# An opening stage with hand-ordered loads and all four weight folds, in a two-layer hybrid diffusion step

## The chip, the cores and the metric

The kernel runs on one core of one Trainium2 chip. The metric is the device time of one execution in microseconds (us); of several runs the median counts. The engines are TensorE (PE in the profile, with its weight loads apart as PEld), VectorE (DVE), ScalarE (ACT), GpSimd (POOL) and SyncE (SP), which issues every data transfer (DMA) of this kernel. Each engine takes its instructions in one order, which is fixed when the program is built.

## What is computed

One inference step with two layers over 1024 latent and 256 context tokens, 1024 wide. Cut to what matters here:

```python
for l in range(2):
    shift, scale, gate = split3(silu(cvec) @ ada_w[l] + ada_b[l])   # for c and for c_ctx
    h = rms_norm(x, norm_g[l]) * (1 + scale) + shift
    if l == 0:   # two attentions: A over all keys, B in a window, both also over cached context keys
        qa, ka, va, ga, qb, kb, vb, gb = split(h @ w_in)
        oa = attention(rope(rms(qa)), rope(rms(ka)), va)
        ob = window_attention(rope(qb), rope(kb), vb, sink)
        y = concat([oa * silu(ga), ob * silu(gb)]) @ w_out
    else:        # Fourier mixing in 4 groups of 256 channels
        u, g = split2(h @ odd_w_in)
        y = (real(fft2(u by group)) * silu(g)) @ odd_w_out
    x = x + gate * y
return rms_norm(x, final_g), new_keys_and_values
```

## The kernel before

**Tiles and precision.** The tokens are ten tiles of 128 rows (0 to 7 latent, 8 and 9 context), in three groups: 0 (tiles 0 to 3), 1 (4 to 7), 2 (8 and 9). Most products are made in three matmuls of high and low parts (hi x hi, hi x lo, lo x hi), so weights and activations are split into a high and a low tile.

**Conditioning.** `cs` holds SiLU of the two conditioning vectors. `ada_load(kk)` fetches four pieces of 512 KB of `ada_w` for layer 0, a chunk of 256 channels; `ada_chunk` multiplies them into a bank and fills scale and shift (`moda`, `modb`) of two of the eight 128-channel blocks k. The other three thirds that are made early (the gate of layer 0, shift and scale of layer 1) come in 24 `ada_step`s of one 512 KB load each, which `ada_fill(n)` issues in portions.

**Weight folds.** The transform of Fourier mixing along a group's 256 channels is multiplied into the projection weights: fold g is `wuT` rows of group g (1 MB) times the constant table `fch`. `fold_load(g)` fetches the rows, `fold_piece(g, kb2)` makes a quarter of the fold: eight matmul records of 256 columns, a copy to a buffer by ScalarE, a store to `wd` in DRAM. `wd` is read much later, in the second layer. Four folds of four pieces are to be made at some time before.

**The opening.** With `EF = 1` fold 0 is made first, its four stores being kept in `later`. Then a loop over the blocks k = 0 to 7 handles group 0: loads of `ada_w`, key weights (at `AT_K`) and query weights (at `AT_Q`), the norm of the group's rows (`norm_rows(0)`, one reciprocal root for all four tiles), `raw_T(0)`, which transposes x into eight banks and copies them to buffers, `mod_chunk` with scale and shift, and, three blocks behind, `gemm_chunk` into four open banks `acc0`: keys and queries of tile pairs 0 and 2. x of groups 1 and 2 is loaded there as well.

The list `S1` then names what follows, in order: `n` norm and `m` modulate a group, `c` cached keys, `K` and `Q` finish an open pair (norm, rotary positions, split), `k` and `q` project a pair and finish it. `AT_N` says how many `ada_step`s go ahead of each. Posts (transposes and stores of a finished pair) are held back two deep (`fl_.depth = 2`). Scratch for finished pairs comes from the buffer kinds in `HZ[0]`.

**Filler in the attentions.** Units of attention A, then of B, run in `attend`; after each, `fl_.pump` gives credit and the filler issues queued work in the order of `ORDER`: query pairs, key pairs of B, fold 1 (`f1`), gate columns. `FLATE = "f2 f3"` puts folds 2 and 3 behind the output weights. Behind these stand the output projection's steps (`proj_load`, `proj_step`), the first four row blocks of which may run inside attention B, once the tiles they read are finished for some units and seven buffers of the kinds u and w are free (`can_run`).

**Who sets the order.** The source order is not the engines' order: a planner at build time lists the instructions by priority in source order, with a timeline of its own, and may put a later ready instruction ahead of an earlier one. Buffers are named rings (`ZONES`: "h" 9, "u" 26, "w" 8, "p" 4, "pt" 3, "q" 2, "e" 4); a load into a buffer waits for that buffer's last reader, and everything behind it on SP waits too. PSUM has eight banks: "s" and "t" three each, "a" and "g" one each.

Matmuls of line 547 in the profile are fold pieces, 471 conditioning, 408 transposes of x, 523 the projections of the opening's loop, 257 all other products in parts, 895 and 967 scores, 1012 and 1018 attention weights and output. Line 831 issues the loads of `ada_step`, 498 those of `ada_load`, 900 the loads of queries from `qd`.

Of the kernel before, what the change touches and what calls it, by code (L numbers as in the profile page):

```python
# [57 lines left out]
ORDER = "qa0 qa1 kb0 qb0 qb1 f1 f0 g0 g1 g2 g3"  # L58
FLATE = "f2 f3"
# [74 lines left out]
def hybrid_step(ctx: ExitStack, tc: tile.TileContext, I, O):  # L134
# [143 lines left out]
    def load_w(src, width=256, tags="w", gap=None, lc=E_WL, each=None):  # L278
        out = []
        for kp in range(2):  # L280
            hi = take(tags, (P, 4, width), F32R)
            lo = take(tags, (P, 4, width), F32R)
            for j in range(2):
# [11 lines left out]
                split(hi[:, 2 * j : 2 * j + 2, :], lo[:, 2 * j : 2 * j + 2, :], raw.a, XE["wh"], lc)  # L295
                drop(raw)
# [95 lines left out]
    def norm_rows(gi):  # L392
        xs = XS[gi]
        n = len(xs)
        ssq = sm.tile([P, 4], F32, tag="ssq", name=f"n{gi}q")
        for i, x in enumerate(xs):
            junk = take("h", (P, D), BF16)
            act.activation(junk.a, x.a, AF.Square, accum_out=ssq[:, i : i + 1])
            drop(junk)
        rs = rsqrt(f"n{gi}r", ssq[:, 0:n], n, 1.0 / D, pw=PW[0])  # L400
        for i, x in enumerate(xs):
            dve.tensor_scalar(x.a, x.a, rs[:, i : i + 1], None, op0=ALU.mult)
# [10 lines left out]

    def raw_T(gi):
        raws = []
        for s in range(4):
            ht = take("u", (P, 2, 512))
            for j in range(2):
                copy("rawT", "ad", ht[:, j, :], x_T(gi, 2 * s + j))
            raws.append(ht)  # L420
        drop(*XS[gi])
        return raws
# [26 lines left out]

    def modulate(gi, lc):  # L450
        h_alloc(gi)
        for k in range(8):
            hh, hl = h_slot(gi, k)
            src = x_T(gi, k)
            tmp = take("h", src.shape)
            mod_chunk(gi, k, src, tmp.a, hh, hl, lc)
            drop(tmp)
        drop(*XS[gi])
# [33 lines left out]
    def ada_load(kk):  # L492
        out = []
        for hb in range(2):
            for part in range(2):
                raw = take(("p", "pt", "q"), (P, 4, 256))
                c0 = part * D + kk * 256
                sp.dma_start(
                    raw.a, I["ada_w"][0, hb * 512 : hb * 512 + 512, c0 : c0 + 256].rearrange("(b p) c -> p b c", p=P)
                )  # L500
                out.append(raw)
        return out

    def ada_chunk(kk, raws):
# [6 lines left out]
        drop(*raws)  # L511

        def fill(tv):
            mod_shift(0, 2 * kk, 2, tv[:, 0:2])
            mod_scale(0, 2 * kk, 2, tv[:, 2:4])

        ada_mods(0, f"modt{kk}", ps, fill)
# [13 lines left out]
    def fold_load(g):  # L531
# [3 lines left out]
        wu = []  # L535
        for j in range(2):
# [4 lines left out]
    def fold_piece(g, kb2, wu, tag="g", later=None):  # L541
        f = fold["f"]
        acc = bank(tag, f"wa{g}{kb2}")
# [6 lines left out]
        wo = take("u" if later is not None else "h", (P, 2, 256))  # L550
        copy("wo", "a", wo.a, acc.rearrange("p (i f) -> p i f", i=2))

        def put():
            rows = slice(kb2 * 256, kb2 * 256 + 256)
            sp.dma_start(wd[g // 2, rows, g % 2, :].rearrange("(k p) f -> p k f", p=P), wo.a)
            drop(wo)

        if later is None:
            put()
        else:  # L560
            later.append(put)
# [7 lines left out]
    early, later = [], []  # L569
    if XF:  # L570
        load_x(0, "u")
    for g in range(EF):
        early.append(fold_load(g))
    if not XF:
        load_x(0, "u")
    for g in range(EF):
        for k in range(4):
            fold_piece(g, k, early[g], "t", later)
    sp.dma_start(gT, I["gT"])
    sp.dma_start(bT, I["bT"])  # L580
    dve.tensor_scalar(bT1, bT[:, :, 8:16], 1.0, None, op0=ALU.add)
    h_alloc(0)
    acc0 = {("k", t): bank("s", f"kv{t}s") for t in (0, 2)}
    acc0.update({("q", t): bank("sa"[t // 2], f"q{t}s") for t in (0, 2)})
    wka = wqa0 = None
    for k in range(8):
        if k % 2 == 0:
            ada = ada_load(k // 2)
        if k == AT_K:
            wka = load_w(w0cols(C_KA), lc=LC0)  # L590
        if k == AT_Q:
            wqa0 = load_w(w0cols(C_QA), lc=LC0)
# [3 lines left out]
        if k == AT_X:  # L596
            load_x(1, "u")
        if k == 0:
            norm_rows(0)
            raws = raw_T(0)  # L600
        if k % 2 == 0:
            ada_chunk(k // 2, ada)
        hh, hl = h_slot(0, k)
        src = raws[k // 2][:, k % 2, :]
        mod_chunk(0, k, src, src, hh, hl, "dp")
        if k % 2 == 1:
            drop(raws[k // 2])
        for j in range(k - GL if k < 7 else k - GL, k - GL + 1 if k < 7 else 8):
            if j < 0:
                continue  # L610
            for nm, at, w in (("k", AT_K, wka), ("q", AT_Q, wqa0)):
                if j >= at:
# [1310 lines left out]
```

## Time and profile before

| what | value |
|---|---|
| median of 3 runs | 1216.64 us (1215.78 to 1218.63) |
| the profiled execution | 1214.73 us |
| its span | 1212.9 us |
| mean granted TensorE clock | 0.991 |
| first matmul (fold 0) | 5.57 us |
| first scores of attention A | 117.37 us |
| fold 1 on TensorE | 445.79 to about 463 us |
| folds 2 and 3 | 705.21 to 743 us |
| first matmul of the output projection | 747.80 us |
| last matmul of attention B | 813.98 us |

A row of the profile's groups gives the line, engine and operation, output and inputs by the program's names, shapes and count; then busy time and the mean of one in ns; then idle time of the engine just before, and what ended it. In the timeline, neighbours of one kind are merged into a row with the start, the length and the count; brackets hold the idle time before and its releaser. In the view of waits a row names who waited, for whom, the total in us, the times and the longest. The view by windows counts, in each stretch, the busy time and the instructions of each engine, the granted clock, the mean busy share of the 16 DMA engines and the GB/s moved. A matmul that stands waiting for its input in the array's pipeline may count as busy.

### The profile page before, as it was taken

Reading aid. Unit: us, or ns where it says so; the run is one execution under the profiler, and the core shown is the slowest. Engines: PE = TensorE matmul, PEld = TensorE weight load, DVE = VectorE, ACT = ScalarE, POOL = GpSimd, SP = SyncE. Lnnn points to the kernel's source line nnn. Section 1 sums busy time; section 2 is a strip of 40 time slices with the busy share of each in tenths; the row PEclk is TensorE's granted clock in tenths of the full one; section 3 lists DMA queues with packets and bytes.
Section 4 is the critical chain, followed back from the end, with each engine's and each line's share of the span. In section 5 each row is a group of like instructions: output and inputs, shape, how many; then the busy total and the mean of one; then the engine's idle time right before and its main releaser. Section 6 shows DMA issues by size and latency. Waiting matters only on the chain. (4 is left out here: it accounts for less than half of the span.)

```text
span 1212.9 us, 22074 instructions
## 1 busy us (share of the span) xinstructions
PE 1162.7 (96%) x8103; PEld 1038.2 (86%) x8103; DVE 842.6 (69%) x1997; ACT 580.5 (48%) x1163; POOL 321.9 (27%) x277
## 2 busy tenths in 40 slices
PE   7879999999999999999999989999999999999997
PEld 5768889999999998999988877877787888997886
DVE  4388888877786785668888867586765953368543
ACT  4352466555565465556667765532365224342211
POOL 2264543503321231010110113311312217344001
PEclk9999999999999999999999999999999999999999
DMA  9947312323524233344343688477214434354321
GB/s 334 369 165 268 88 59 76 93 86 98 139 60 132 78 112 92 91 124 123 84 122 102 190 211 237 150 235 211 103 39 141 153 113 141 123 191 159 122 103 54
DMA packets 129328, 168.81 MB, mean 139 GB/s; under 512 B 26298, under 2 KB 86454, under 8 KB 129220
## 3 DMA queue, kind: packets, MB, share of 16 engines
q1 hardware_dynamic: 129220, 167.40, 44.3%
q8 instruction: 64, 1.05, 0.4%
q14 instruction: 44, 0.36, 0.1%
HBM read 123.19 MB, written 44.16 MB: 138 GB/s over the span
## 5 line engine op out<-in xcount | busy, mean ns | idle before, releaser
L1015 DVE TENSOR_TENSOR pt<-pt,pt 128x512 fp32r<-128x512 f32 (+1 forms) x264 | 170.3, 658 | 45.5 <-ACT pt L269 44.9
L269 ACT ACTIVATE pt<-pt 128x512 fp32r<-128x512 f32 (+1 forms) x264 | 146.2, 576 | 87.9 <-PE pt L1012 55.9
L1018 PE MATMUL av<-pt,u 128*128 128x256 f32 x1008 | 169.9, 290 | 0.6 <-DVE e L1029 0.3
L1012 PE MATMUL pt<-identr,p 128*128 128x128 f32 x1008 | 155.0, 273 | 3.1 <-DVE pt L1015 1.6
L1018 PEld LDWEIGHTS av<-pt,u 128*128 128x128 f32 x1008 | 140.3, 189 | 5.1 <-DVE pt L1015 0.9
L257 PE MATMUL q<-w,u 128*128 128x256 f32 x864 | 132.8, 289 | 1.5 <-DVE u L433 1.5
L1012 PEld LDWEIGHTS pt<-identr,p 128*128 128x128 f32 x1008 | 118.6, 141 | 9.6 <-DVE pt L1015 2.6
L257 PE MATMUL ga<-u,w 128*128 128x512 f32 (+1 forms) x576 | 124.2, 360 | 0.1
L257 PEld LDWEIGHTS q<-w,u 128*128 128x128 f32 x864 | 116.1, 191 | 6.2 <-DVE u L433 1.9
L936 ACT ACTIVATE p<-p,nm 128x1280 f32<-128x1280 f32 (+1 forms) x80 | 95.3, 1191 | 53.3 <-DVE p L929 49.8
L257 PEld LDWEIGHTS ga<-u,w 128*128 128x128 f32 x576 | 93.8, 188 | 14.2 <-ACT pt L269 0.3
L275 POOL TENSOR_TENSOR w<-h,w 128x512 fp32r<-128x512 f32 x42 | 56.9, 1370 | 128.4 <-DVE w L271 92.8
L895 PE MATMUL sL<-u,q 128*128 128x512 f32 x256 | 81.8, 412 | 4.6 <-DMA q<-qd 4.6
L275 POOL TENSOR_TENSOR u<-h,u 128x512 fp32r<-128x512 f32 x24 | 35.2, 1473 | 141.5 <-ACT u L269 111.2
L895 PE MATMUL sC<-u,q 128*128 128x256 f32 x320 | 63.3, 298 | 6.6 <-DMA q<-qd 6.5
L936 ACT ACTIVATE p<-p,NM 128x640 f32<-128x640 f32 (+2 forms) x80 | 59.1, 739 | 17.9 <-DVE p L929 17.6
L257 PE MATMUL oz<-u,u 128*128 128x512 f32 x224 | 61.7, 398 | 1.8 <-DVE h L1219 1.3
L929 DVE TENSOR_SCALAR_CACHE_REDUCE p<-sL 128x512 f32<-128x512 f32 x64 | 43.8, 684 | 24.0 <-PE sL L895 13.5
L671 POOL TENSOR_TENSOR h<-h,rope 128x512 f32<-128x512 f32 (+1 forms) x18 | 21.3, 1183 | 141.1 <-ACT h L754 91.1
L895 PEld LDWEIGHTS sC<-u,q 128*128 128x128 f32 x320 | 48.3, 189 | 10.1 <-issue 7.5
L257 PE MATMUL kv<-w,u 128*128 128x256 f32 x384 | 56.5, 287 | 0.0
L1027 ACT ACTIVATE e<-av 64x256 f32<-64x256 f32 x80 | 30.5, 382 | 46.1 <-PE av L1018 40.0
(742 smaller groups left out, 2580.3 us busy)
## 6 DMA issues: line engine op xcount, KB each, us to landing
q<-qd SPq DMA_DIRECT2D x80, 256.0 KB
h<-i_w_in SPq DMA_DIRECT2D x40, 256.0 KB
p<-i_ada_w SPq DMA_DIRECT2D x19, 512.0 KB
h<-i_w_out SPq DMA_DIRECT2D x32, 256.0 KB
pt<-i_ada_w SPq DMA_DIRECT2D x15, 512.0 KB
qd<-q SPq DMA_DIRECT2D x22, 256.0 KB
q<-i_ada_w SPq DMA_DIRECT2D x10, 512.0 KB
u<-g1d SPq DMA_DIRECT2D x9, 512.0 KB
```

What stands on the lines that cost most here:

```text
L257: pe.matmul(out, a, b, start=i == 0, stop=i == n - 1)
L269: act.activation(out, in_, AF.Copy)
L275: pick("lo" + lc, lc).tensor_sub(dst_l, src, dst_h)
L671: pick("rope", XE["rope"]).tensor_mul(t1.rearrange("p t h (b c) -> p t (h b) c", b=2), y.rearrange("p t h (b c) -> p t (h b) c", b=2), cb)
L895: pe.matmul(ps, q_at(q, s, hc), keys, start=s == 0, stop=s == 1)
L929: dve.tensor_scalar(p[i][:, end[i] : end[i] + n], ps, sign, last[i], op0=ALU.mult, op1=ALU.min, accum_out=c)
L936: act.activation(p[i][:, 0 : end[i]], p[i][:, 0 : end[i]], AF.Exp, bias=last[i], scale=-1.0, accum_out=SU[:, t, hd + i, 0:1],)
L1012: pe.transpose(tp[:, jj * 256 + i * P : jj * 256 + i * P + P], p[i][:, off : off + P], ident)
L1015: dve.tensor_sub(pt[:, 1, 0:n], tp[:, 0:n], pt[:, 0, 0:n])
L1018: pe.matmul(acc, vv, pt[:, s, jj * 256 : jj * 256 + 256], start=c + jj + s == 0, stop=c + jj == nt - 1 and s == 1,)
L1027: act.activation(lo_sb.a, a3[64:128], AF.Copy)
```

## The change

The opening is written as a list of steps, `PH0`, whose loads SP issues in exactly this order (`manual_schedule` for SP; the other engines keep the planner's order). All four folds are in it (`EF = 4`), and the filler of both attentions has none. Keys of tile pairs 0, 2, 4 and 6 accumulate in the four open banks while groups 0 and 1 are modulated block by block; queries of pairs 0 and 2 move to the second list, and the query pair of tiles 8 and 9 to the filler of attention A. x of group 0 is transposed and modulated from the bank, with no copy between. Rows are normalised one by one in group 0, two by two in the others. `wuT` is loaded in halves, and the folds' stores are eight of 512 KB.

In `PH0`, `f` loads a fold, `F` makes a piece, `G` stores half a fold, `x` loads and `N` normalises a group, `L`, `A` and `M` load, multiply and finish a conditioning chunk, `T` transposes a block of group 0 ahead, `X`, `Y` and `Z` modulate a block of group 0, 1 and 2, `w` loads a weight (0 keys, 1 queries) and `s` splits it, `S` loads small tables, `K` and `R` accumulate block i for pairs 0, 2 and 4, 6. In `S1`, `I` finishes an open key pair, `a` issues conditioning steps, `P` runs held posts down to the last, `c`, `k`, `q` are as before.

```diff
-S1 = "c1 n2 m1 c0 m2 K0 Q0 Q2 K2 k6 q8 k4 k8".split()
-E_ML = ("p", "d")
+PH0 = """f0 S0 x0 N0 f1 L0 F00 F01 F02 F03 f2 w0 L1 F10 F11 F12 F13 f3 x1 A0 T0 T1 s0 F20 M0 F21 X0 X1 T2 F22 F23 L2 N1 K0 K1
+ A1 T3 F30 M1 G00 G01 G10 G11 L3 X2 X3 F31 K2 F32 K3 F33 Y0 R0 Y1 R1 w1 S1 T4 A2 x2 N2 Y2 T5 M2 R2 G20 G21 G30 G31 X4 Y3 X5 R3
+ K4 Y4 K5 A3 T6 Y5 M3 R4 X6 T7 R5 X7 Y6 K6 Y7 K7 R6 R7"""
+S1 = """s1 S2 V Z0 Z1 c0 I0 a2 Z2 Z3 c1 I2 a1 q0 P Z4 Z5 I4 a2 P Z6 Z7 I6 a1 q2 P a2 P k8 a2 P a3 P a9 P"""
+S1_H = "h"
+E_ML = ("dp", "dp", "d")
-EF = 1
+EF = 4
-ORDER = "qa0 qa1 kb0 qb0 qb1 f1 f0 g0 g1 g2 g3"
-FLATE = "f2 f3"
+ORDER = "qa0 qa1 kb0 qb0 qb1 g0 g1 g2 g3"
+FLATE = ""
...
     def norm_rows(gi):
         xs = XS[gi]
-        n = len(xs)
+        n = 1 if gi == 0 else 2
...
-        wu = []
-        for j in range(2):
-            wu.append(take("w", (P, 1024)))
-            sp.dma_start(wu[j].a, I["wuT"][(2 * g + j) * P : (2 * g + j + 1) * P, :])
+        wu = [take("w", (P, 1024)) for j in range(2)]
+        for h in range(parts):
+            cols = slice(h * (1024 // parts), (h + 1) * (1024 // parts))
+            for j in range(2):
+                sp.dma_start(wu[j][:, cols], I["wuT"][(2 * g + j) * P : (2 * g + j + 1) * P, cols])
...
+        if first:
+            if kb2 % 2 == 0:
+                early[g, kb2 // 2] = take("u", (P, 4, 256))
+            wo = early[g, kb2 // 2][:, 2 * (kb2 % 2) : 2 * (kb2 % 2) + 2, :]
...
+    def mod_T(gi, k, lc):
+        if k == 0 and gi > 0:
+            h_alloc(gi)
+        hh, hl = h_slot(gi, k)
+        src = XT.pop((gi, k)) if (gi, k) in XT else x_T(gi, k)
+        tmp = take("h", src.shape)
+        mod_chunk(gi, k, src, tmp.a, hh, hl, lc)
+        drop(tmp)
+        if k == 7:
+            drop(*XS[gi])
...
+        elif nm in "KR":
+            t = 4 * "KR".index(nm)
+            gemm_chunk(acc0[t], t, W[0], i)
+            gemm_chunk(acc0[t + 2], t + 2, W[0], i)
...
+    region = tc.manual_schedule(engines={sp.engine})
+    region.__enter__()
+    for op in PH0.split():
+        first_step(op)
+    wka, wqa0 = W[0], W[1]
+    region.__exit__(None, None, None)
...
-    HZ[0] = ("h", "q", "pt", "p")
+    HZ[0] = S1_H
     XE.update(XE1)
     fl_ = Filler()
-    fl_.depth = 2
+    fl_.depth = 9
```

More of the change, by code (lines that the diff above doesn't have):

```diff
@@ L275, in split, with load_w @@
         pick("lo" + lc, lc).tensor_sub(dst_l, src, dst_h)
-    def load_w(src, width=256, tags="w", gap=None, lc=E_WL, each=None):
+    def load_w(src, width=256, tags="w", gap=None, lc=E_WL, each=None, later=None):
         out = []
@@ L495, in ada_load @@
             for part in range(2):
-                raw = take(("p", "pt", "q"), (P, 4, 256))
+                raw = take(tags, (P, 4, 256))
                 c0 = part * D + kk * 256
@@ L511, in ada_chunk, with ada_fin @@
         drop(*raws)
[L513 to L517, printed above, removed]
+        rows[kk] = take("e", (P, P))
+        act.activation(rows[kk].a, ps[:, 0:P], AF.Copy)
+    def ada_fin(kk):
+        row = rows.pop(kk)
+        tp = t_bank(f"modt{kk}")
+        pe.transpose(tp[:, 0:P], row.a, ident)
+        drop(row)
+        tv = tp[:, 0:P].rearrange("p (j v) -> p j v", j=4)[:, :, 0:2]
+        mod_shift(0, 2 * kk, 2, tv[:, 0:2])
+        mod_scale(0, 2 * kk, 2, tv[:, 2:4])
     def gemm_chunk(acc, t, w, k):
@@ L549, in fold_piece @@
                 )
[L550 to L559, printed above, removed]
-        else:
-            later.append(put)
+        if first:
+            if kb2 % 2 == 0:
+                early[g, kb2 // 2] = take("u", (P, 4, 256))
+            wo = early[g, kb2 // 2][:, 2 * (kb2 % 2) : 2 * (kb2 % 2) + 2, :]
+        else:
+            wb = take("h", (P, 2, 256))
+            wo = wb.a
+        copy("wo", "a", wo, acc.rearrange("p (i f) -> p i f", i=2))
+        if not first:
+            fold_put(g, kb2 * 256, wo)
+            drop(wb)
         if kb2 == 3:
@@ L567, in fold_piece, with small_loads @@
                 del fold["f"]
[L569 to L581, printed above, removed]
-    h_alloc(0)
[L583 to L592, printed above, removed]
+    h_alloc(0)
+    acc0 = {t: bank("sssa"[t // 2], f"kv{t}s") for t in (0, 2, 4, 6)}
+    W, ada, wu0, w_fin = {}, {}, {}, {}
+    def small_loads(i):
+        if i == 0:
+            sp.dma_start(gT, I["gT"])
+            sp.dma_start(bT, I["bT"])
+            dve.tensor_scalar(bT1, bT[:, :, 8:16], 1.0, None, op0=ALU.add)
+        elif i == 1:
             sp.dma_start(rope, I["rope"])
@@ L595, in hybrid_step @@
             sp.dma_start(gq, I["gq"].partition_broadcast(P))
[L596 to L612, printed above, removed]
-                    for i in range(0 if j == at else j, j + 1):
-                        for t in (0, 2):
-                            gemm_chunk(acc0[nm, t], t, w, i)
@@ L1078, in out_weights @@
         return out
-    order = [nm for nm in ORDER.split() if nm not in [f"f{g}" for g in range(EF)]]
+    order = [nm for nm in ORDER.split()]
     base = {"qa": C_QA, "qb": C_QB, "kb": C_KB, "g": C_G}
@@ L1120, in hybrid_step @@
                 work.append((5.4, lambda t=t, nm=nm: kv_pair(1, t, ws[nm], "g"), ("kb", t)))
-        elif nm[0] == "f":
-            for k in range(4):
-                work.append((FC, lambda k=k, nm=nm, j=j: fold_piece(j, k, ws[nm])))
         elif i < len(order) - 2:
@@ L1129, in hybrid_step @@
             fl_.add(*w)
-        if i < len(order) - 2 and nm[0] != "f":
+        if i < len(order) - 2:
             fl_.add(0.0, releaser(nm))
@@ L1141, in hybrid_step @@
     wout_next(len(wk_left))
-    for nm in FLATE.split():
-        fl_.add(0.0, loader(nm))
-        for k in range(4):
-            fl_.add(FC, lambda k=k, nm=nm: fold_piece(int(nm[1]), k, ws[nm]))
     lastA = {g: (NT - 1, g, 1) for g in range(2)}
@@ L1370, in hybrid_step, with late_fold, fn @@
     steps = [(i, j) for i in range(5) for j in range(2)]
-    for n, ij in enumerate(steps):
+    def late_fold(nm):
+        def fn():
+            ws[nm] = fold_load(int(nm[1]))
+            return 0
+        return fn
+    for n, nm in enumerate(FLATE.split()):
+        fl_.add(0.0, late_fold(nm))
         if n == 0:
             fl_.add(0.0, lambda: proj_load(0, 0), ready=can_run(0, 0))
+        for k in range(4):
+            fl_.add(FC, lambda k=k, nm=nm: fold_piece(int(nm[1]), k, ws[nm]))
+    if not FLATE:
+        fl_.add(0.0, lambda: proj_load(0, 0), ready=can_run(0, 0))
+    for n, ij in enumerate(steps):
         if n == 8:
```

170 lines of the change are left out of this document (97 added, 73 removed).

## Prediction, made before the changed kernel was run

> **What bounds the kernel now.** I read the page first: its share of busy time, then the chain that ended last (8% of the span, all in the last stage, so it says nothing of the stages that change). TensorE is nearly always busy, and its work is the same before and after. So only TensorE time that is idle or stretched can go, and I looked for where that is.
>
> ```profile
> span 1212.9 us, 22074 instructions
> PE 1162.7 (96%) x8103; PEld 1038.2 (86%) x8103; DVE 842.6 (69%) x1997; ACT 580.5 (48%) x1163; POOL 321.9 (27%) x277
> ...
> PE 8%; DVE 0%; DMA 0%; issue 0%; POOL 0%; POOLq 0%; DVEq 0%
> ```
>
> The view of busy time by windows, for the stages that the change touches (columns: window, length, busy time of PE, PEld, DVE, ACT, POOL, granted clock, DMA share, GB/s):
>
> ```profile
> 0.00:60.00 60.00, 47.39 (x468) 38.82 (x469) 23.32 (x61) 22.87 (x41) 15.77 (x20) 0.94 1.02 352
> 61.00:79.00 18.00, 14.01 (x122) 12.06 (x124) 15.76 (x24) 12.77 (x22) 12.54 (x10) 1.00 0.26 90
> 60.00:117.00 57.00, 50.68 (x658) 44.86 (x658) 45.27 (x110) 21.45 (x42) 29.85 (x29) 1.00 0.67 234
> 0.00:117.00 117.00, 98.07 (x1124) 83.68 (x1125) 68.59 (x170) 44.32 (x83) 45.62 (x49) 0.97 0.85 294
> 445.00:457.00 12.00, 12.00 (x80) 10.93 (x79) 8.47 (x21) 7.52 (x13) 4.00 (x4) 1.00 0.66 214
> 705.00:748.00 43.00, 36.50 (x220) 32.49 (x219) 32.41 (x91) 26.34 (x60) 10.13 (x5) 0.96 0.90 248
> ```
>
> The first 60 us are bound by transfers (DMA share 1.02 at 352 GB/s) while VectorE is busy 23 of 60 us. Then 18 us follow in which transfers nearly stop (0.26) and VectorE is busy 15.8 of 18. At 445 to 457, where fold 1 runs, TensorE has no gap. At 705 to 748, where folds 2 and 3 run, it has gaps of 6.5 us although the folds are there as filler.
>
> The busy time of the opening flatters TensorE, since a matmul that waits counts as busy. Its true work I get from rows in which one kind runs without a break (timeline of PE; columns: start, length, line, output and inputs, shapes, count):
>
> ```profile
> 5.57 9.42 PE L547 MATMUL wa<-h,w 128*128 128x256 f32 x32 [5.57 <-DMA w<-i_wuT]
> 14.92 0.41 PE L471 MATMUL ada<-p,e 128*32 128x128 f32 x4
> 20.78 2.53 PE L408 MATMUL xt<-identr,u 128*128 128x128 f32 x20
> ...
> 56.21 0.39 PE L471 MATMUL ada<-p,e 128*32 128x128 f32 x4
> ...
> 98.16 0.65 PE L471 MATMUL ad<-pt,e 128*32 128x128 f32 x16
> 98.62 0.62 PE L471 MATMUL ad<-p,e 128*32 128x128 f32 x16
> 99.06 0.62 PE L471 MATMUL ad<-pt,e 128*32 128x128 f32 x16
> 99.61 0.74 PE L257 MATMUL q<-w,u 128*128 128x256 f32 x4
> ...
> 111.66 5.87 PE L257 MATMUL kv<-w,u 128*128 128x256 f32 x48
> 117.37 0.39 PE L895 MATMUL sL<-u,q 128*128 128x512 f32 x1
> ...
> 741.52 1.89 PE L547 MATMUL wa<-h,w 128*128 128x256 f32 x8
> 743.06 0.82 PE L895 MATMUL sC<-u,q 128*128 128x256 f32 x4
> ...
> 747.80 5.86 PE L257 MATMUL oz<-u,w 128*128 128x512 f32 x24 [0.53 <-ACT h L269]
> ```
>
> From starts: a fold piece takes 743.06 - 741.52 = 1.54 us, so a fold of four pieces 6.2; the projection of a pair of tiles 117.37 - 111.66 = 5.7; 48 conditioning matmuls 99.61 - 98.16 = 1.45, so 0.03 each; a transpose 0.12. The opening up to the first scores at 117.4 then holds: fold 0 6.2; four conditioning chunks of 64, 7.7; 80 transposes 9.7; eight pairs 45.7; 24 conditioning steps of 16, 11.6; small transposes about 4 (an estimate from the 0.12). Sum 85, so 32 us of the 117.4 are lost.
>
> **The change part by part.**
>
> 1. *First attention.* Fold 1 leaves (-6.2), and the query pair of tiles 8 and 9 comes in from the opening (+5.7). TensorE has no gap there (row 445 to 457), so both count fully: **-0.5 us**. ScalarE copies a fold piece out in the opening instead of here; it was busy 7.5 of 12 us, so that is worth nothing.
>
> 2. *End of the second attention.* Folds 2 and 3 leave: 2 x 6.2 = 12.3 us of TensorE, four loads and eight stores of 4 MB in all. The waits of PE from 680 to 800 and the clock beside the longest of them:
>
> ```profile
> PE sC L895 <- DMA q<-qd: 6.5, 4, 3.4
> ...
> 715.58 0.47 PE L895 MATMUL sC<-u,q 128*128 128x256 f32 x2 [3.41 <-DMA q<-qd]
> ...
> 716.00:725.00 9.00, 8.14 (x48) 7.34 (x47) 5.20 (x15) 4.72 (x11) 4.72 (x2) 0.81 0.69 213
> ```
>
> The waits are for query loads, in a stretch with a DMA share of 0.90, where the folds' 4 MB compete; 6.5 us could go with them. Against that, VectorE is busy 32.4 of the 43 us without any fold work, so attention alone cannot go through in 43 - 12.3 = 30.7 us. The next filler is the output projection, whose first row block needs only query tile 0, long finished, and free buffers, of which the folds held four; it can move up. Its own gate holds the later blocks: the fourth needs tile 6. Bounds: -18.8 (folds and all query waits) to +1.7 (nothing gained, one more gap like that at 712 with its low clock, 9 x 0.19). I take **-11**: nearly the folds' time, with the 1.3 us lost to VectorE at the end, where the filler is short, and the query waits left as they are, as the projection's loads take the folds' place in the queue.
>
> 3. *Loads of the opening.* Sizes from the page's DMA issues:
>
> ```profile
> h<-i_w_in SPq DMA_DIRECT2D x40, 256.0 KB
> p<-i_ada_w SPq DMA_DIRECT2D x19, 512.0 KB
> ...
> u<-i_x SPq DMA_DIRECT2D x8, 512.0 KB
> ...
> wd<-h SPq DMA_DIRECT2D x12, 256.0 KB
> ```
>
> They give, up to the load of the last conditioning chunk: folds 4.5 MB, x 4.2, conditioning 8.4, key weights 1.0, half of the fold stores 2.1, together 20.2 MB: 57 us at 352 GB/s. With query weights, tables, the last x and the other stores 24.8 MB: **70 us**. Before, the last chunk was in by about 55.5 (its last matmuls, row 56.21). SP issues eight more fold loads, of half the size, and eight stores of 512 KB for sixteen of 256; while the transfers are the bound, that costs nothing. What was in the queue's way after 61 us:
>
> ```profile
> SPq L831 <- PE ad L471: 17.1, 1, 17.1
> ...
> 61.45 0.46 SPq L663 DMA_DIRECT2D h<-i_cv  x1
> 79.14 1.92 SPq L831 DMA_DIRECT2D p<-i_ada_w  x2
> ```
>
> SP stood 17.1 us behind a load whose buffer was not free. The hand order puts loads that can go in this place; the 24 steps of 0.5 MB (12.6 MB, 36 us) follow from 70 to 106.
>
> 4. *Compute of the opening.* New TensorE work: folds 24.7, chunks 7.7, 64 transposes 7.7, four key pairs 22.8, small 1 = 64 us before the last key accumulation, against 57 us until the last chunk lands plus its chain. The folds' first loads are halved (0.75 MB instead of 1.3 MB to the first matmul), which I put at -1 of the 5.57 us. So this part ends near 74 (69 if TensorE never waits, 82 if the chain after the last chunk is bare). VectorE has room there: it gains the modulation of the second group's eight chunks, some 8 us by the rows below (half of each x8, and four subtractions that POOL did), in a stretch where it was busy 23 of 60. After that: 16 transposes 1.9, steps 11.6, three pairs 17.1, small 3.5 = 34 us of TensorE, 36 us of loads, and of VectorE 45.3 (row 60 to 117) less those 8 and one query pair, some 6: 31 us. I take 40, the largest of these with some latency. The copies of the raw transposed rows vanish (2.7 us of VectorE); the norms, in seven groups for three, add four times one instruction of VectorE and one of POOL at 1.03 us. Both lie beside the loads, with POOL busy 15.8 of 60: nothing. Longer scratch lists without "p", "pt", "q" could make posts wait: from nothing to the 1.9 us of the nearest wait in a query post here, counted in the 40. First scores at 74 + 40 = 114 instead of 117.4: **-3.4** (bounds -12 at 105, +13 at 130).
>
> ```profile
> L432 DVE TENSOR_SCALAR h<-xt,moda,modb 128x512 f32<-128x512 f32 (+1 forms) x8 | 5.4, 669 | 0.5 <-ACT u L431 0.5
> L429 DVE CAST u<-h 128x512 fp32r<-128x512 f32 (+1 forms) x8 | 5.2, 647 | 1.6 <-ACT h L428 1.6
> ...
> L271 DVE COPY u<-xt 128x512 f32<-128x512 f32 x4 | 2.7, 685 | 0.9 <-PE xt L408 0.9
> ...
> 15.45 1.03 POOL L236 TENSOR_TENSOR n0ry<-n0rx,mhalf 128x4 f32<-128x4 f32 x1 [13.61 <-DVE n0rx L234]
> ...
> DVE h L686 <- POOL qn08rsy L238: 1.9, 1, 1.9
> ```
>
> Sum: -0.5 - 11 - 3.4 = -14.9 us, I say -14.5. The profiled execution took 1214.7 us with its span of 1212.9, 1.9 under the median 1216.6 of the runs shown. So 1200.2 by the profile, **1202** as a median.
>
> [...]
>
> **The rivals.**
>
> *A. The folds filled time that is idle anyway.* For it: VectorE at 32.4 of 43 us, and gaps with the folds still in. Against: the projection stands ready. If the gate holds the projection back, the 6.5 us of gaps stay and one more stretch of low clock comes (1.7), so of the 12.3 us some 4 are won in place of 11: time 1209.
> [...]
>
> *B. The opening packs well.* Transfers never stop and the second half takes its 34 to 36 us: first scores near 106, -8 more: time 1194.
>
> *C. The opening grows by what it takes in.* Its loss stays 32 us, as chains (norm, transpose, modulate, project) set it: 85 + 18.5 - 5.7 + 32 = 130, +12.4 instead of -3.4: time 1217.5, the same as before.
>
> *D. Slower: one held load stops the whole hand-ordered queue.* The loads for x group 2 reuse buffers that conditioning chunk 2 gives back, chunk 3's load those of chunk 1; behind them in SP's order stand eight stores' second half, and the modulation's last output buffers are those stores' sources. A fold piece ahead of the chunk on TensorE waits for a load of the same queue. Price: a hold like the 17.1 us above, and a query-like wait of 3.4 behind it, 20.5: time 1222. It is slower than before from a hold of 17 us on. Against it: each such buffer's reader stands well ahead in the list, and nine conditioning buffers serve four loads at a time.
>
> **How the numbers follow.** Forecast 0.47 (1195 to 1208), A 0.19, B 0.14, C 0.09, D 0.11. The range of 8 in 10 leaves out the best half of B and most of D and takes in the edge of C: 1190 to 1217. About 0.2% (2.4 us) is what a measurement here can tell from no change. Faster: forecast, A, B, 0.80; same: C, 0.09; slower: D, 0.11.
>
> **What would show it.** Right: DMA share near 1 to about 70 us and no gap of 17 us on SP; first scores at 109 to 119; no fold matmul after 85 us; the first projection matmul in attention near 705 or earlier on the old clock instead of 747.8; the distance from first scores to the end of attention shorter by 9 to 14 us. Wrong: SP waiting over 5 us for one load in the first 70 us, first scores after 125, or new idle TensorE at VectorE's hand between 690 and 800.

## The result, and the profile after

The changed kernel is **slower by 0.5%**: 1221.85 us as the median of 18 runs beside 1215.38 for the kernel before, ratio 1.0049 with a 95% interval of 1.0036 to 1.0062. That is outside the forecast range of 1190 to 1217. The profiled execution took 1226.76 us, 4.9 above the kernel's own median, so its gap of 12 us to the profile of before is about twice the gap of the medians (6.5). The stage lengths below add up to the 12, and part of each belongs to that one execution.

Head of the page of the changed kernel:

```profile
span 1225.0 us, 22081 instructions
PE 1169.1 (95%) x8103; PEld 1045.0 (85%) x8103; DVE 837.6 (68%) x2000; ACT 578.4 (47%) x1159; POOL 318.2 (26%) x278
```

TensorE has the same 8103 recorded matmuls as before, so the question is again where it is idle or stretched. I cut the span at marks that every version has: the start of the 51st value product (in steady attention A), of the 641st (the border to attention B), and of the last matmul of the output projection. The view by windows between these marks, for the kernel before (columns as in the prediction):

```profile
0.00:170.03 170.03, 148.40 (x1523) 130.77 (x1524) 115.55 (x273) 71.22 (x132) 78.43 (x78) 0.97 0.66 223
170.03:525.57 355.54, 350.79 (x2665) 333.23 (x2664) 262.55 (x636) 203.47 (x364) 86.40 (x81) 1.00 0.33 96
525.57:881.05 355.48, 342.27 (x2021) 298.60 (x2020) 272.71 (x719) 193.36 (x429) 66.60 (x40) 1.00 0.55 158
```

and for the changed kernel:

```profile
0.00:179.96 179.96, 164.22 (x1603) 146.85 (x1604) 111.72 (x274) 75.86 (x139) 74.48 (x77) 0.96 0.74 245
179.96:533.38 353.42, 348.03 (x2649) 331.18 (x2648) 262.70 (x637) 201.00 (x358) 89.49 (x85) 1.00 0.32 91
533.38:892.82 359.44, 334.68 (x1958) 290.59 (x1956) 271.17 (x723) 190.16 (x423) 64.83 (x40) 0.98 0.51 144
```

Length less PE busy is TensorE's idle time in a stage. **Opening**: 9.9 us longer; TensorE's busy time grew by 15.8 and its idle time shrank only from 21.6 to 15.7. **Attention A**: 2.1 shorter. **Attention B with the projection**: 63 recorded matmuls and 7.6 us of busy time fewer, and yet 4.0 longer, as idle time went from 13.2 to 24.8. The two folds are 12.3 us of work; busy time fell by less, as the granted clock was lower, 0.98 in that row for 1.00 before. The rest, in the second layer, is alike (331.9 and 332.2).

The opening in detail, changed kernel, view by windows (the first part up to the last key accumulation, and the second up to the first scores):

```profile
0.00:60.00 60.00, 50.10 (x388) 40.72 (x392) 17.23 (x45) 24.10 (x43) 12.68 (x20) 0.97 1.01 342
60.00:88.00 28.00, 28.00 (x285) 26.12 (x286) 19.86 (x40) 12.60 (x21) 13.51 (x12) 1.00 0.87 297
88.00:133.00 45.00, 39.16 (x544) 35.30 (x543) 38.66 (x99) 14.14 (x33) 24.50 (x25) 0.92 0.74 242
```

and its timeline of PE, from the first folds to the first scores. Its line numbers are its own: 557 fold pieces, 467 conditioning, 516 transposes of scale and shift, 526 the projections of the first list; further on 924 scores, 1041 and 1047 attention weights and output, 1044 and 1058 VectorE's evictions behind these two (two less in the versions with other lists of steps):

```profile
5.27 9.20 PE L557 MATMUL wa<-h,w 128*128 128x256 f32 x32 [5.27 <-DMA w<-i_wuT]
15.07 7.14 PE L557 MATMUL wa<-h,w 128*128 128x256 f32 x32 [0.60 <-DMA w<-i_wuT]
22.14 0.41 PE L467 MATMUL ada<-p,e 128*32 128x128 f32 x4
...
50.27 3.62 PE L557 MATMUL wa<-h,w 128*128 128x256 f32 x16
...
69.26 0.39 PE L467 MATMUL ada<-p,e 128*32 128x128 f32 x4
...
77.70 0.27 PE L516 MATMUL modt<-identr,e 128*128 128x128 f32 x1
...
87.96 0.64 PE L526 MATMUL kv6s<-w,u 128*128 128x256 f32 x4
...
132.80 1.22 PE L924 MATMUL sL<-u,q 128*128 128x512 f32 x2
```

The first conditioning matmul stands behind two whole folds and starts at 22.14; before, it started at 14.92. The last conditioning chunk is multiplied at 69.26 and its scale and shift are transposed at 77.70. From 60 to 88 TensorE has no gap at all. Before, the last transpose of scale and shift started at 59.23; it now comes 18.5 us later. The second part takes 45 us, and VectorE is busy for 38.7 of them: the modulation that was to go beside the loads came late, so that VectorE was busy 17.2 us in the first 60 (23.3 before).

At the end of attention B the view of waits (who waited, for whom, us in total, times, longest) shows new waits of TensorE for VectorE; from 533 to 893 in the changed kernel:

```profile
PE av L1047 <- DVE e L1058: 7.2, 4, 3.5
PE pt L1041 <- DVE pt L1044: 5.7, 8, 1.9
PE sC L924 <- DMA q<-qd: 3.9, 1, 3.9
```

In the kernel before, from 525 to 882:

```profile
PE sC L895 <- DMA q<-qd: 6.5, 4, 3.4
PE pt L1012 <- ACT e L997: 1.5, 2, 1.3
PE oz L257 <- DVE h L1219: 1.3, 1, 1.3
PE pt L1012 <- DVE pt L1015: 1.1, 2, 0.9
```

The query wait is smaller by 2.6 us, and 12.9 us of waits for VectorE's evictions stand where 1.1 stood.

### The profile page after: what moved, and what is told of

Same layout as the page of the kernel before. It is cut to its first block, busy times and chain, and to the rows that moved or that the text cites. A ratio compares the mean times of both kernels' runs of the same rounds, so it can differ in the third digit from the quotient of the medians.

```text
span 1225.0 us, 22081 instructions
## 1 busy us (share of the span) xinstructions
PE 1169.1 (95%) x8103; PEld 1045.0 (85%) x8103; DVE 837.6 (68%) x2000; ACT 578.4 (47%) x1159; POOL 318.2 (26%) x278
## 3 DMA queue, kind: packets, MB, share of 16 engines
q8 instruction: 64, 1.05, 0.4%
## 5 line engine op out<-in xcount | busy, mean ns | idle before, releaser
L263 PE MATMUL q<-w,u 128*128 128x256 f32 x960 | 144.2, 289 | 0.0
L263 PEld LDWEIGHTS q<-w,u 128*128 128x128 f32 x960 | 127.3, 190 | 4.3 <-issue 0.2
L263 PEld LDWEIGHTS ga<-u,w 128*128 128x128 f32 x576 | 93.6, 188 | 17.2 <-ACT pt L275 1.6
L281 POOL TENSOR_TENSOR w<-h,w 128x512 fp32r<-128x512 f32 x38 | 50.3, 1341 | 140.3 <-DVE w L277 106.4
L281 POOL TENSOR_TENSOR u<-h,u 128x512 fp32r<-128x512 f32 x21 | 28.9, 1382 | 146.6 <-ACT u L275 146.6
L263 PE MATMUL oz<-u,w 128*128 128x512 f32 x224 | 62.4, 405 | 2.9 <-ACT w L275 2.0
L263 PE MATMUL of<-u,u 128*128 128x512 f32 x176 | 57.9, 395 | 0.1
L958 DVE TENSOR_SCALAR_CACHE_REDUCE p<-sC,nsink 128x256 f32<-128x256 f32 x80 | 37.5, 473 | 27.6 <-PE sC L924 24.1
```

Source lines behind the costliest of these rows:

```text
L263: pe.matmul(out, a, b, start=i == 0, stop=i == n - 1)
L281: pick("lo" + lc, lc).tensor_sub(dst_l, src, dst_h)
L958: dve.tensor_scalar(p[i][:, end[i] : end[i] + n], ps, sign, last[i], op0=ALU.mult, op1=ALU.min, accum_out=c)
```

## The experiments

Two theories stood at the start. **Theory 1**: a fold costs its TensorE time in the opening and lies in idle time at the end of attention B. **Theory 2**: the rebuilt list itself lengthens the opening, a fold costs the same in either place, and the end of B is bound by TensorE's work.

The versions differ in the folds that the opening makes (`EF`), the folds at the end of B (`FLATE`), and the place of the query pair of tiles 8 and 9. All stage lengths in us, each from one profiled execution, between the marks above; the ratios are to the kernel before. The last column says by how much that execution lay above or below the median of its own kernel:

| version | folds in opening, in A, in B | query pair 8/9 | opening | A | B and projection | ratio of medians | profiled execution less median |
|---|---|---|---|---|---|---|---|
| before | 1, 1, 2 | opening | 170.0 | 355.5 | 355.5 | 1 | -0.7 |
| after | 4, 0, 0 | A | 180.0 | 353.4 | 359.4 | 1.0049 | +4.9 |
| no_hand | 4, 0, 0 | A | 181.5 | 350.5 | 358.1 | 1.0043 | +2.6 |
| after_pm | 4, 0, 0 | A | 176.6 | 350.6 | 363.8 | 1.0114 | -1.9 |
| dup_b | 4, 0, 2 again | A | 177.1 | 349.6 | 358.2 | 1.0029 | -0.2 |
| nomm_open | 2 and 2 without matmuls, 0, 0 | A | 172.0 | 347.7 | 357.1 | 0.9947 | +0.7 |
| ef3 | 3, 0, 1 | A | 171.3 | 347.9 | 365.9 | 1.0071 | -4.7 |
| ef2 | 2, 0, 2 | A | 171.6 | 347.0 | 356.1 | 0.9974 | -2.9 |
| ef2_q8 | 2, 0, 2 | opening | 178.8 | 353.6 | 360.5 | 1.0108 | -1.7 |
| ef1 | 1, 0, 3 | A | 163.2 | 347.7 | 363.9 | 0.9949 | +0.5 |
| ef1_pm | 1, 0, 3 | A | 163.3 | 348.0 | 369.2 | 0.9956 | +5.9 |
| ef1_q8 | 1, 0, 3 | opening | 170.3 | 351.8 | 362.0 | 1.0021 | +0.2 |
| ef0 | 0, 0, 4 | A | 167.6 | 352.1 | 374.4 | 1.0077 | +4.1 |
| nomm_b | 1, 1, 2 without matmuls | opening | 169.6 | 355.5 | 355.4 | 1.0032 | -4.8 |

Four kernels have the opening of the changed one or nearly so (after, dup_b, after_pm, and no_hand but for SP's order): 176.6 to 181.5, with a mean of 178.8. So a stage of one profile is good to a few us.

**ef2: folds 2 and 3 back to the end of B.** The steps `f`, `F` and `G` of these folds are struck out of `PH0`.

```diff
-EF = 4
+EF = 2
-FLATE = ""
+FLATE = "f2 f3"
```

> The changed kernel with folds 0 and 1 in the opening and folds 2 and 3 again at the end of attention B, as before. Theory 1 (a fold costs its full TensorE time of 6.2 us in the opening and lies in idle time at the end of attention B): first scores 12 us earlier than 132.8, so at about 120; attention B no longer than the 293 us it takes now; time about 1222 - 12 = 1210. Theory 2 (the rebuilt list itself lengthens the opening, and a fold costs its time wherever it stands): first scores stay at 130 to 133, attention B becomes 12 us longer; time 1222 to 1234.

Measured: 1211.8 us, ratio 0.9974 (0.9952 to 0.9996). The opening is 8.4 us shorter than the changed kernel's, and attention B with the two folds in it is 3.4 shorter than without them. That is Theory 1 in kind and not in size: two folds are 12.3 us of TensorE work, and first scores came at 125.7 where about 120 was expected.

**nomm_open: the matmuls of folds 2 and 3 left out in the opening**, with loads, copies and stores kept.

```diff
-        acc = bank("t" if first else "g", f"wa{g}{kb2}")
-        for i in range(2):
+        acc = wu[0][:, 0:512] if first and g > 1 else bank("t" if first else "g", f"wa{g}{kb2}")
+        for i in range(0 if first and g > 1 else 2):
```

> The changed kernel with the matmuls of folds 2 and 3 left out; their loads, copies and stores stay in the opening (ScalarE copies a piece of the loaded rows). Theory 1: only TensorE time goes, 12.3 us, and first scores come at about 120, time about 1210. Theory 2: TensorE is not what sets the opening, first scores at 130 or later, time 1219 to 1222.

Measured: 1210.24, 0.9947 (0.9923 to 0.9971). The openings of nomm_open and of ef2, by windows:

```profile
0.00:172.03 172.03, 151.56 (x1532) 134.13 (x1533) 110.36 (x273) 74.25 (x138) 75.51 (x77) 0.97 0.78 256
0.00:171.59 171.59, 154.09 (x1540) 134.07 (x1541) 113.00 (x274) 71.16 (x131) 75.14 (x77) 0.97 0.71 232
```

The opening is as short without the matmuls as without the whole folds (172.0 and 171.6; first scores at 124.2 and 125.7). So what the two folds cost there is their TensorE time, some 7 us of it against the mean of 178.8; 4 MB of loads and stores and eight copies by ScalarE cost nothing that can be seen beside it.

**dup_b: the changed kernel makes folds 2 and 3 a second time at the end of B.**

```diff
-FLATE = ""
+FLATE = "f2 f3"
-            if fold["n"] in (EF, 4):
+            if fold["n"] in (4, 6):
```

> The changed kernel that makes folds 2 and 3 a second time at the end of attention B (their loads, matmuls, copies and stores are all doubled). Theory 1: these 12.3 us of TensorE lie in idle time there, so the time stays within 3 us of 1222. Theory 2: TensorE bounds attention B, so the time goes up by 12 to about 1234.

Measured: 1219.24, 1.0029 (1.0003 to 1.0055), no slower than the changed kernel (1.0049). 12.3 us of TensorE work, four loads and eight stores were added and cost nothing that can be seen. Attention B of dup_b:

```profile
526.77:884.93 358.16, 342.83 (x2022) 299.11 (x2020) 274.84 (x722) 193.29 (x431) 65.78 (x40) 0.99 0.54 157
```

Its idle time is 15.3 us where the changed kernel has 24.8.

**no_hand: the list without the hand-made order of SP's queue.**

```diff
-    region = tc.manual_schedule(engines={sp.engine})
-    region.__enter__()
...
-    region.__exit__(None, None, None)
```

> The changed kernel without the hand order of SP: the planner orders the loads of the opening. Theory 1: the folds' work sets the opening's end, so first scores stay within 4 us of 132.8 and the time within 4 us of 1222. Theory 2 in the form that the fixed order of the loads holds the conditioning chain back: the third and fourth scale and shift come before the 65 and 78 us of the changed kernel by 8 us or more, first scores by about 125, time about 1214.

Measured: 1221.57, 1.0043 (1.0026 to 1.0060), the same as with it. The third and fourth scale and shift come at 70.1 and 81.0, later than the 65.5 and 77.7 of the changed kernel and not earlier, and first scores at 135.5. SP's order by hand is not what costs, nor does it bring anything that can be seen here.

**ef1 and ef3: one and three folds in the opening.**

```diff
-EF = 4
+EF = 1
-FLATE = ""
+FLATE = "f1 f2 f3"
```

(ef1; in ef3 the values are 3 and "f3". The steps of the folds that leave are struck out of `PH0`.)

> The changed kernel with fold 0 alone in the opening and folds 1, 2 and 3 at the end of attention B. Theory 1 (two folds took 8 us from the opening and nothing from attention B): the opening ends another 3 to 4 us earlier; attention B stays at 291 to 295 us if its idle time holds a third fold, and grows by up to 6 if it doesn't. Time 1207 to 1214. Rival (the gain of the run with two folds came from where loads fell, not from TensorE's work): no order by the number of folds, 1212 to 1222.

> The changed kernel with folds 0, 1 and 2 in the opening and fold 3 at the end of attention B. Theory 1: between the two, opening about 4 us shorter than with four, attention B the same, time about 1217. Rival: no order by the number of folds.

Measured: ef1 1208.63, 0.9949 (0.9933 to 0.9965), which beats both kernels; ef3 1223.9, 1.0071 (1.0045 to 1.0097). ef1 goes Theory 1's way, though in other sizes: its opening is 8.4 us shorter than that of ef2 (3 to 4 were expected), and its B 7.8 longer. ef3 doesn't. Its opening is no longer than that of ef2, where the granted clock was 0.97; in ef3 it was 0.99 (0.02 of 171 us make 3.4). Its loss is at the end of B, which has one fold and takes 365.9. The waits of PE there and the window that they fall in, of ef3:

```profile
PE av L1045 <- DVE e L1056: 7.9, 3, 4.6
```

```profile
800.00:820.00 20.00, 9.89 (x48) 7.51 (x45) 15.97 (x33) 7.14 (x13) 0.00 (x0) 0.73 0.82 240
```

TensorE was busy for half of these 20 us, at a clock of 0.73, with 7.9 us of waits in B for VectorE to take a finished value product out. So the end of B can be 10 us longer than in ef2 with one fold fewer in it, in idle time (23.5 us for 12.9) and at a lower clock (0.96 over the stage for 0.99). That it comes from the way in which the engines' orders interlock is likely and not shown. Neither theory foresaw it.

**nomm_b: the kernel before, without the matmuls of folds 2 and 3 at the end of B.**

```diff
-        acc = bank(tag, f"wa{g}{kb2}")
-        for i in range(2):
+        acc = wu[0][:, 0:512] if g > 1 else bank(tag, f"wa{g}{kb2}")
+        for i in range(0 if g > 1 else 2):
```

> The kernel before with the matmuls of folds 2 and 3 left out at the end of attention B; their loads, copies and stores stay (ScalarE copies a piece of the loaded rows). Theory 1 (they lie in idle time there): the time stays within 3 us of the kernel before, 1213 to 1217. Rival, as the prediction had it (TensorE bounds that stage): 9 to 12 us less, 1204 to 1207.

Measured: 1219.23, 1.0032 (1.0012 to 1.0052): no gain, rather a small loss. The window of attention B in nomm_b:

```profile
525.04:880.48 355.44, 334.11 (x1958) 289.89 (x1956) 273.60 (x722) 193.75 (x429) 65.39 (x40) 0.98 0.54 158
```

Against the row 525.57 to 881.05 of before: 63 recorded matmuls and 8.2 us of busy time are gone, and the length is the same to 0.04 us. That agreement is luck: the profiled execution is the lowest of ten, 4.8 us below their median, and by the medians nomm_b is 0.3% slower. Either way nothing of the 12.3 us was won. 8.1 us turned into idle time, and the rest is matched by a lower clock, 0.98 for 1.00 (0.02 of 355 us make 7, part of it in the gaps). One stretch of nomm_b at half clock, and the one before it:

```profile
806.85:810.27 3.42, 1.03 (x6) 0.75 (x7) 3.42 (x11) 0.65 (x2) 0.00 (x0) 1.00 0.90 320
810.27:820.51 10.24, 7.31 (x20) 5.66 (x21) 9.05 (x17) 4.07 (x6) 2.64 (x2) 0.50 0.67 194
```

The waits show at whose hand TensorE was idle:

```profile
PE sC L895 <- DMA q<-qd: 7.0, 2, 5.7
PE av L1018 <- DVE e L1029: 4.2, 3, 2.1
PE pt L1012 <- DVE pt L1015: 2.7, 4, 1.2
```

The query wait of before (6.5) didn't go, though the folds' loads and stores are still there, so this run can't say what those do; and 6.9 us of waits for VectorE's evictions stand where 1.1 stood. This is the plainest answer to the prediction's second step.

**ef2_q8 and ef1_q8: the query pair of tiles 8 and 9 back at the end of the opening.**

```diff
-S1 = """ ... q2 P a2 P k8 a2 P a3 P a9 P"""
+S1 = """ ... q2 P a2 P k8 a2 P q8 a3 P a9 P"""
-                if nm == "qa0" and t in (0, 2):
+                if nm == "qa0" and t in (0, 2, 8):
```

> The kernel with two folds in the opening, with the query pair of tiles 8 and 9 projected at the end of the opening again and not in attention A. If its 5.7 us of TensorE cost the same on both sides: the same time as with two folds (1212), within 2 us, the opening longer and attention A shorter by about 5. If the opening is bound by other engines there: the opening grows by more than 8 us or by less than 3 us.

> The rebuilt opening with fold 0 alone (folds 1 to 3 at the end of attention B) and with the query pair of tiles 8 and 9 put back at the end of the opening: the same work as the kernel before has there, in the new order. Theory of added work (the opening is as long as its TensorE work makes it, whatever the order of loads): the pair costs the 7 us that it cost beside fold 1, the 51st value product of attention A starts near 170 as before (163 without the pair), the time is 1215 to 1218. Rival, that the hand-made order itself gained the 7 us of the run with fold 0 alone: the 51st value product at 163 to 166, the time 1208 to 1211.

Measured: ef2_q8 1228.54, 1.0108 (1.0076 to 1.0141); ef1_q8 1217.39, 1.0021 (1.0005 to 1.0037). With the pair in the list the opening is 7.2 us longer in both. Openings of ef1 and of ef1_q8, by windows:

```profile
0.00:163.15 163.15, 144.63 (x1501) 127.42 (x1502) 111.29 (x273) 68.37 (x126) 75.19 (x77) 0.97 0.70 232
```

```profile
0.00:170.34 170.34, 148.72 (x1525) 130.56 (x1525) 115.81 (x277) 67.83 (x127) 77.39 (x78) 0.96 0.67 223
```

The second does the work that the kernel before does in its opening, in the new order, and ends within 0.3 us of it (170.03), with nearly the same TensorE time (148.7 and 148.4) and number of projection matmuls (576 and 575). So the rebuilding with its order of loads gained **nothing** that these runs can tell from zero (the same opening differs by 4.9 us between the four kernels above), and the 6.9 us of ef1 go with the pair. They aren't the pair's own TensorE time: ef1 has 561 projection matmuls up to the mark, ef2 563 and ef2_q8 575, only 15 and 12 fewer without the pair (1.8 and 1.4 us at 0.12 each), since other query work takes its place ahead of the mark. What the rest of the 7.2 us is stays open.

What the pair costs in A was expected wrongly, too: with its 48 matmuls no longer in the filler, A is not shorter but longer by 4.1 and 6.6 us. In both, 21 more gate matmuls of 512 columns came into A (165 for 144), for 15 and 12 query matmuls of 256 columns. Of the 6.6 us of ef2_q8, 4.4 are idle time, and TensorE's waits for query loads have grown; the waits of PE in A, of ef2 and then of ef2_q8:

```profile
PE sL L922 <- DMA q<-qd: 1.7, 3, 0.9
```

```profile
PE sL L922 <- DMA q<-qd: 5.2, 5, 1.6
PE sC L922 <- DMA q<-qd: 1.0, 1, 1.0
```

Why these loads come later stays open.

**ef0: no fold in the opening.**

```diff
-EF = 4
+EF = 0
-FLATE = ""
+FLATE = "f0 f1 f2 f3"
```

> No fold at all in the opening, all four at the end of attention B. Theory of added work: the opening is shorter by about 5.5 us (the mean of the three steps from one fold to four), the 51st value product at 157 to 158, the four folds (some 24 us of TensorE) still lie in idle time of attention B, the time near 1203. Rival 1: without folds the opening waits for loads and VectorE, the 51st value product stays near 163. Rival 2: the idle time in B (some 13 to 25 us) is used up by three folds, the fourth costs its 6 us there, the time stays at 1208 to 1210.

Measured: 1223.96, 1.0077 (1.0052 to 1.0102). It went the way of both rivals, and further than the price of either: the 51st value product came at 167.6 (rival 1 had 163), and the time is 14 us above rival 2's. First 20 us, ef0 and then ef1:

```profile
0.00:20.00 20.00, 7.16 (x73) 4.17 (x73) 5.79 (x19) 6.68 (x12) 4.61 (x13) 1.00 0.89 297
```

```profile
0.00:20.00 20.00, 12.37 (x76) 9.64 (x76) 4.50 (x17) 8.01 (x15) 3.47 (x12) 1.00 0.91 299
```

Fold 0 lies in the time in which TensorE waits for the first loads; without it, TensorE is idle there and the opening is not shorter (167.6 against 163.2). At the other end, the windows of attention B of ef1 and ef0:

```profile
510.89:874.79 363.90, 350.25 (x2053) 307.92 (x2052) 272.33 (x723) 196.10 (x435) 64.66 (x40) 0.99 0.54 160
```

```profile
519.70:894.14 374.44, 358.40 (x2085) 313.45 (x2084) 276.51 (x723) 198.37 (x439) 65.67 (x39) 0.98 0.56 162
```

Idle time is 13.6 and 16.0 us, no less than the 13.2 of before. Without any fold in B it is 20 to 25 us (after, no_hand, nomm_b, nomm_open), so the first two seem to use up what can be used (ef2_q8, with two, still has 21.7). Beyond that, idle time in the stage doesn't make a fold free: the third and the fourth lengthen it, to 362 to 364 and 374 from the 355 to 361 of the versions with two. How much the third costs is uncertain, 7.8 us between ef2 and ef1 and 1.5 between ef2_q8 and ef1_q8.

**after_pm and ef1_pm: the last gate products on GpSimd.** In the changed kernel VectorE stood 4.4 us behind a row of denominators that was still on its way, ahead of evictions of value products, a theory for the lost time in B:

```profile
DVE u L1216 <- DMA u<-scd: 4.4, 2, 4.3
```

```diff
-XE3 = {"wh": "a", "pm": "d", "xa": "d"}
+XE3 = {"wh": "a", "pm": "p", "xa": "d"}
```

> The changed kernel with the last gate products of the projection inputs on GpSimd instead of VectorE. Theory: the end of attention B is set by VectorE standing in order behind a gate product whose row of denominators is still on its way (VectorE idle 4.4 us for scd and 0.9 for gd at that line, TensorE idle 7.2 us at the eviction of value products behind it). Then VectorE's waits for these transfers go, TensorE's wait for that eviction falls below 3 us, the stretch from the start of attention B's value products to the 241st projection matmul falls from 302 to about 297, the time to about 1217. Rival: the wait only hands over to the next (GpSimd needs 2.4 us for a product instead of 1.2 and the projection waits for it), the stretch stays at 300 or more, the time at 1220 to 1224.

> The same edit on the version with fold 0 alone in the opening, where VectorE is idle 5.7 us in all at these products (1.7, 1.6, 1.4, 1.0). Theory: the stretch from the start of attention B's value products to the 241st projection matmul falls from 307 to about 301, the time from 1208.6 to about 1203. Rival: no change or up to 3 us more, 1208 to 1212. A third view, that every edit draws the interleaving at the end of B anew between some 296 and 309 us: this stretch changes, but without relation to VectorE's waits for these transfers.

Measured: after_pm 1228.14, 1.0114 (1.0092 to 1.0136); ef1_pm 1208.88, 0.9956 (0.9938 to 0.9974). **The theory fell.** VectorE's wait for the row is gone, and TensorE's wait for the eviction isn't; waits of PE in after_pm, 527 to 895:

```profile
PE av L1047 <- DVE e L1058: 8.0, 3, 3.5
PE eoE L1269 <- DVE q L1365: 5.0, 1, 5.0
PE sC L924 <- DMA q<-qd: 4.3, 1, 4.3
```

The eviction wait is 8.0 in place of 7.2, and 5.0 us for VectorE at the first transposes behind the projection are new. after_pm is 6.3 us slower than the changed kernel by the medians, its stage 4.4 longer, worse than the rival's 1220 to 1224. ef1_pm is where its rival had it: the medians are 0.3 us apart, and the 5.3 us by which its stage is longer come from the slowest of its ten executions.

## Why the prediction was wrong, point by point

**Step 2, the end of attention B (forecast -11, bounds -18.8 to +1.7): wrong, and the main error.** It took the stage as bound by TensorE's work, so that "nearly the folds' time" would go. The profile of after has +4.0, and nomm_b, which removes the same matmuls and nothing else, -0.04 in the stage and +0.3% in the median. The rival that the folds fill idle time was right, and went further than its own price of 4 us won. The row quoted for the opposite had it in view: 36.5 of 43 us busy with the folds *in*, and VectorE busy for 32.4. If attention alone can't go through faster than VectorE and the query loads let it, taking filler out makes gaps; that this is the limit is argued from the waits and not shown by a run of its own. The step saw this and set the output projection against it as the next filler. The projection did move up, from 747.80 to 730.57 (722.8 on the old clock, counted from the border to attention B), but not to 705, and TensorE still waited. The clock was a term that the step put at nothing in its forecast: in nomm_b the stretch from 810.27 to 820.51, which has gaps, ran at 0.50 of it, and the stage lost 8.1 us to idle time and some 7 to the clock, in part the same us, against the 12.3 that left.

**Step 4, the compute of the opening (forecast -3.4, bounds -12 to +13): wrong.** First scores came at 132.8, beyond the bound, and by the firmer mark of the 51st value product the opening grew by 9.9. The rival that the opening grows by what it takes in put them at 130, on the argument that its loss of 32 us stays. This is what the runs show: with the pair out of the list, three more folds cost 15.6 us (163.2 to the mean of 178.8), 5.2 each against the row's 6.2, though unevenly from one to the next; ef1_q8 shows that the new order removes none of the loss. The rival's own sum comes out by another way, as the pair's 5.7 us didn't leave: the changed kernel has recorded eight pairs' worth of projection matmuls before its first scores, as many as before (384). So 85 + 18.5 = 103.5 us of work stand in 132.8, and 29 are lost (32 before).

The steps of that sum that failed were two. The first part, 64 us of TensorE beside 57 us of loads, was to end near 74. At the prediction's own prices (0.19 for a fold's matmul, 0.12 for a projection's or a transpose, 0.03 for a conditioning matmul) the matmuls recorded in the first 60 us make 40 us of work, an estimate; the other 27, with half a query pair that came ahead of its place, fill the stretch from 60 to 88.5. The last chunk's matmuls ended at 69.6 and its transposition came 8 us later, in a queue of TensorE without gaps, so the part ended at 88.6. And the second part was to take 40 us with VectorE at 31; it took 44, and VectorE was busy for 38.7 of the 45 in the row.

**Step 3, the loads (70 us at full rate): the rate held, and the last chunk's loads landed nearly in time.** The first windows of the changed kernel:

```profile
0.00:20.00 20.00, 14.13 (x55) 11.87 (x56) 4.50 (x17) 9.20 (x17) 3.46 (x12) 1.00 0.89 296
20.00:40.00 20.00, 17.50 (x142) 13.50 (x141) 5.86 (x13) 5.31 (x9) 5.46 (x4) 0.91 1.07 363
40.00:60.00 20.00, 18.46 (x195) 15.35 (x197) 6.87 (x15) 9.59 (x17) 3.76 (x4) 1.00 1.08 367
```

They moved 20.5 MB in 60 us; the sum of 20.2 MB up to the last chunk would have been through at 59. SP issued the last chunk's four loads from 48.77 to 53.95, and by the trace's record of their landings the last was in at 61.7, 5 us after the 57 of the forecast. Its matmuls ran from 64.10 to 69.65, and none of them stands in the view of waits as waiting for a load: TensorE, busy without a gap from 60 on, was late for them. SP had no hold of 17 us. Its longest in the first 130 us was 4.7, total and times in this row of the changed kernel's waits:

```profile
SPq L849 <- PE ad L467: 12.0, 7, 4.7
```

So the rival "slower by one held load" had the sign and not the mechanism.

**Step 1, attention A (forecast -0.5): the sign held.** The changed program shows -2.1, with -5.0 and -5.9 in no_hand and dup_b, whose A has the same content. What failed is the +5.7 for the pair: against before, the A of all three has the fold's 32 matmuls less and only 12 query matmuls more (637 for 625), so that its work falls by 6.2 - 1.4 = 4.8 us.

**The rivals were put as alternatives and came together.** Folds free at one end and an opening that keeps its loss are independent of each other: +9.9 with nothing won at B is the result, of one execution that lay 4.9 us above its median. Neither was given a joint price, and the range was cut at the edge of one of them.

**The tests named.** DMA share near 1 to 70 us (1.01 to 60, 1.05 from there) and no long hold: right. No fold matmul after 85 us: right (the last ended at 54). First scores at 109 to 119, the projection near 705 on the old clock, and a way from first scores to the end of attention that is 9 to 14 us shorter: all three wrong (132.8, 722.8, and 3.5 us shorter to the last value product). Two of the signs of failure came true, first scores after 125 and idle TensorE at VectorE's hand.

**What stays open.** Why the end of B takes 366 us in ef3 with one fold and 355 to 361 in most with none or two; the runs show that the waits are for VectorE's evictions and that removing VectorE's wait for one kind of transfer doesn't remove them, not what does. Why the opening is 7 us longer with the query pair in its list, when up to the mark it has 1.4 to 1.8 us more projection work. Each stage was seen in one execution per version, and the same stage differs by some 5 us between versions that have the same program in it.

## What to carry to other kernels

Before filler is moved out of a stage, look at TensorE's idle time in that stage *with* the filler in. Where gaps stand beside it, the filler may be free there, and taking it out may only give gaps and a lower clock (in nomm_b 8.1 us of idle time, and 0.98 for 1.00). Gaps alone don't prove it: ef1 has 13.6 us of idle time beside three folds, and its third fold is not free. The plainest test is to leave the matmuls out and see whether the time moves. A place has a limited amount of such room, here about two folds at the end of B and one at the very start, as far as one profile of each version tells. The best version (ef1, 0.5% faster than before) fills the start, takes the query pair out of the opening's list, and pays for a third fold in B.

A rebuilt stage is best split into its order and its content by a run that has the new order with the old content: here that run ended 0.3 us from the old one, within the few us by which one profile differs from the next.

## What the runs showed of the hardware

The clock that was granted fell where TensorE's waits crowded: 0.73 in the 20 us of ef3 in which TensorE was busy for 9.89 us, while it was 1.00 in attention A (the rows 170.03 to 525.57 and 179.96 to 533.38). So some us of waits at the end of B may cost more than their own length. The longest wait of TensorE beside that 0.73 was 4.6 us, but it took no such length: in the kernel before, a single gap of 1.9 us stands ahead of a stretch at half clock.

```profile
126.17:129.58 3.41, 1.51 (x10) 1.06 (x10) 2.81 (x7) 1.69 (x5) 0.00 (x0) 1.00 0.49 176
129.58:133.00 3.42, 3.42 (x17) 3.19 (x16) 3.30 (x10) 2.31 (x5) 0.41 (x1) 0.51 0.68 185
```

In the traces of the kernel before and of the changed one the half-clock stretches between 10 and 1195 us last 3.41, 6.83 or 10.24 us. They begin 13 times out of full clock, and TensorE had then been busy for 0.18 to 0.62 of the 3.41 us before. On the same grid of 3.41 us, there are 11 stretches at full clock in which it was busy for less than 0.47, and all were followed by half clock; of the 19 in which it was busy for 0.51 to 0.70, two were. A gap of 2.32 us (84.06 to 86.38, kernel before) lies across two of these stretches, busy for 0.64 and 0.68, and full clock went on; one of 1.06 us (110.63 to 111.69, changed kernel) is the longest in a stretch busy for 0.42, and half clock followed. So in these two traces it was the busy share of 3.41 us that went with the clock, more than the length of one gap.

The record of a matmul can hold a wait: at 34.25 in the kernel before, one starts together with its weight load of 0.19 us and takes 0.38 us, while the median of the 48 into that bank is 0.28. The length of the first fold there, 9.4 us busy, has more to it: its first ten matmuls took 0.63 to 0.77 us each, and the twenty from 10.5 us on 0.38.

The transfers reached 367 GB/s in the changed kernel (row 40 to 60), with loads of mostly 256 and 512 KB and stores of 512 KB.
